# First stage of an attention and mLSTM step kept back and emitted in one stated order; first loads split, prompt compressed with a unit of the samples

## The chip, the cores and the metric

The kernel runs on one core of a Trainium2 chip. The metric is the device time of one execution in microseconds. Five engines work side by side and each takes its instructions in the order in which they stand: PE (matmul, with its weight loads shown as PEld), DVE, ACT, POOL, and SP, which here only issues DMAs. ACT issues some DMAs as well.

## The reference, cut to what matters

A two-layer decoder step: native sparse attention, then an mLSTM. It is done for a prompt of 512 tokens and for 8 samples of one new token with 1024 cached tokens each. Only the start of the first layer matters here: the norm of the input, one projection to keys and values, and the compression of the keys and values of the "cmp" branch into summaries.

```python
SEQ, DEC_BATCH, PAST_LEN, CMP_BLK, CMP_STRIDE = 512, 8, 1024, 32, 16

def compress_branch(rows, pe, w1, b1, w2):
    # block i covers rows [16 i, 16 i + 32); summary = W2 silu(W1 flatten(rows + pe) + b1)
    seg = rows.reshape(B, n_seg, CMP_STRIDE, 2, N_KV_HEADS, HEAD_DIM)
    w1r = w1.reshape(2, CMP_R, CMP_STRIDE, HEAD_DIM, CMP_HID)
    part = einsum('bnrchd,cjrde->bnjche', seg, w1r)
    hid = einsum('cld,clde->ce', pe, w1) + b1
    for j in range(CMP_R):
        hid = hid + part[:, j:j + n_cmp, j]
    return einsum('bnche,ced->bnchd', silu(hid), w2)      # kc for c = 0, vc for c = 1

def nsa_project(h, w_in):
    p = h @ w_in          # q, 4 cached and 2 window key/value groups, gates, z
```

All of it is float32. For the prompt `rows` are its own 512 projected rows, for the samples 1024 rows from pages of the cache.

## The kernel before

Every float32 product is made of three products of the faster format: each operand is split into `hi` (a rounding copy, mostly on ACT) and `lo` (operand minus `hi`, `lo_of`, line 310, on DVE or POOL), and `mm3` (lines 313 to 315) adds `whi*xhi`, `whi*xlo` and `wlo*xhi` in one PSUM bank. So no product can be finished before both splits are there.

The 520 tokens (512 of the prompt and 8 samples) are two column halves `c` of 260. The first stage has these parts:

- **Loads and norm.** ACT issues the first weight tile and both halves of x (`x_t`); `split_x` (371, 372) writes `hhi` and `hlo` for each of eight kt and multiplies by the norm's weight; the squares `sq` (647 on POOL, 649 on ACT) are summed over partitions by a product with `ones` (650), sixteen in all. `rms_factor` makes `rr` from the sum.
- **Key and value tiles.** `kv_tile(i)`, i = 0 to 11: 24 matmuls of 260 columns for each half c, into the two `mm` banks, scaled by `rr` (534) into `kvt`. Weights come through `load_w` (whi, wlo).
- **Sample units.** `cmp_unit(b, c)`, sample b = 0 to 7, keys (c = 0) or values (c = 1): eight pages of the cache by SP (`praw`, three buffers), split into `phi` and `plo` in two parts k, and 48 matmuls of 256 columns with the two halves of w1 (`w1h`, `w1l`) into an `s` bank; then a sigmoid on ACT, `hs`, and a second product (516) that is made during the next unit. `load_w1` loads w1, splits it and sums `acc` over sixteen small DVE instructions (449, 451), from which the bias `hcst` comes.
- **The prompt's compression.** `cmp_prompt_pack` (565) packs `xp` out of two key or value tiles; `cmp_prompt(c)` splits it (574) and makes 48 matmuls of 128 columns into a `t` bank. c = 0 stands after the seventh sample unit, c = 1 after the last.
- **End.** `gates`, `cmp_out`, and then the second stage, which begins with `q_tile`.

In this stage the order is written out for SP alone: it issues in the order of the code. On PE, DVE, ACT and POOL a scheduler of the language places the instructions. Later stages are recorded and emitted in an order given by tables of numbers. Which engine makes a `lo` is set by strings, one letter for each:

```python
LO_W1 = "GGGG"
LO_PG = "VVVVVVVVVVVVVVVVVVVVVVGVVVVVVVVV"
SQX = "SGSGSGSGSGSGSGSS"
```

Of the kernel before, what the change touches and what calls it, by code (L numbers as in the profile page):

```python
# [9 lines left out]
F32 = mybir.dt.float32  # L10
# [8 lines left out]
CH = 260  # L19
# [30 lines left out]
FIRST = 11  # L50
# [130 lines left out]
)  # L181
KSC = float(np.float32(512.0 ** -0.5))
# [52 lines left out]

def const_layout():
# [31 lines left out]
def step_kernel(ctx, tc, ap):  # L268
    nc = tc.nc
    V, S, G, PE, SP = nc.vector, nc.scalar, nc.gpsimd, nc.tensor, nc.sync  # L270

    E = {"V": V, "G": G, "S": S}
    mctx0 = ctx.enter_context(ExitStack())
    mctx0.enter_context(tc.manual_schedule(engines={mybir.EngineType.SP}))
    const = ctx.enter_context(tc.tile_pool(name="const", bufs=1))
    wctx = ctx.enter_context(ExitStack())
    wp = wctx.enter_context(tc.tile_pool(name="wstream", bufs=2, side="right"))
    ps = ctx.enter_context(tc.tile_pool(name="ps", bufs=1, space=PSUM))
# [89 lines left out]
    def split_x(c, kt, xs, li):  # L368

        nwc = nw[:, li, kt:kt + 1]  # L370
        S.activation(hhi[c][:, kt], xs, AF.Copy, scale=nwc)  # L371
        return V.scalar_tensor_tensor(hlo[c][:, kt], xs, nwc, hhi[c][:, kt].bitcast(F32),  # L372
                                      op0=OP.mult, op1=OP.subtract)
# [12 lines left out]
    kvp = l0.enter_context(tc.tile_pool(name="kvp", bufs=1))  # L386
# [16 lines left out]
    hp_ = hctx.enter_context(tc.tile_pool(name="hp", bufs=1, side="right"))  # L403
# [31 lines left out]
    def load_w1(c, after=None):  # L435
        acc = cp.tile([128, 128], F32, name="acc", tag="acc")
        w1[c] = []
        for j in range(2):
            hi = cp.tile([128, 8, 128], F32R, name="w1h", tag="w1h", bufs=3)
            lo = cp.tile([128, 8, 128], F32R, name="w1l", tag="w1l", bufs=3)  # L440
            w1[c].append((hi, lo))
            raw = wp.tile([128, 8, 128], F32, name="wraw", tag="wraw", bufs=WRAW)
            SP.dma_start(raw, ap["w1"][:, c, j])
            S.activation(hi, raw, AF.Copy)
            lo_of(lo, raw, hi, E[LO_W1[2 * c + j]])
            with tc.issue_after(after) if after else nullcontext():
                for r in range(8):
                    if j == 0 and r == 0:
                        V.tensor_scalar(acc, raw[:, r], pe[:, c, j, r:r + 1], None, op0=OP.mult)
                    else:  # L450
                        V.scalar_tensor_tensor(acc, raw[:, r], pe[:, c, j, r:r + 1], acc, op0=OP.mult, op1=OP.add)
# [4 lines left out]

# [6 lines left out]
    def pages(row, u, dst, col, n):  # L463

        for i in range(8):
            v = SP.value_load(pt[0:1, row, u * 8 + i:u * 8 + i + 1], min_val=0, max_val=79)
            SP.dma_start(dst(i), ap["cache"][bass.ds(v, 1), :, col:col + n].rearrange("o p f -> (o p) f"))

    def cmp_unit(b, c):
# [4 lines left out]
        parts = {}  # L474

        def split(k):
# [3 lines left out]
            rv = raw[:, :, k * 128:(k + 1) * 128].rearrange("p g (x s) -> p x g s", s=8)  # L480
# [2012 lines left out]
```

## Time and profile before

| | |
|---|---|
| runs, us | 1149.37, 1151.88, 1156.47; median 1151.88 |
| profiled execution, us | 1150.31, its span 1148.6 |
| mean granted PE clock | 0.976 |
| PE, PEld, DVE, ACT, POOL busy | 93%, 82%, 71%, 54%, 23% of the span |
| first product of a q tile | at 226.8 us |

The profile is one execution. Its page gives the busy share of each engine, then the span in 40 slices of 28.7 us with the busy share in tenths and the clock that PE was granted. Other answers of the trace give the busy time in a stretch, groups of instructions by source line, waits ("A <- B" is the time in which A was idle until B was done), single instructions in order of time, and the DMA engines' load.

### The profile page before, as it was taken

To read this page: it belongs to the slowest core of one execution; us is meant where nothing else is said; L and a number is where in the kernel's file an instruction comes from. 1 tells how busy PE (TensorE), PEld (TensorE's weight loads), DVE (VectorE), ACT (ScalarE), POOL (GpSimd) and SP (SyncE) were. 2 spreads that over 40 slices of the span, in tenths; PEclk is the share of its full clock that TensorE was granted. 3 is DMA by queue.
4 is the path that set the end of the run, shared out by engine and by line. 5 is a ranking of instruction groups with operands and counts; after the bars stand their busy time and mean duration, and the time that the engine had idled before them with its cause. 6 is when DMAs were issued, how large, how long until landed. Compare 5 with 4: busy or idle time off the path is not lost.

```text
span 1148.6 us, 24240 instructions
## 1 busy us (share of the span) xinstructions
PE 1071.7 (93%) x8673; PEld 939.2 (82%) x8673; DVE 812.1 (71%) x1970; ACT 616.7 (54%) x1304; POOL 262.8 (23%) x298
## 2 busy tenths in 40 slices
PE   5899999999999899999899998989989999999985
PEld 4899999999988767778889988779956687877885
DVE  5675564488468888875776667676665778778786
ACT  5533444434567777763444444567655656655644
POOL 5021212042300100002341221221231333322111
PEclk9998999999999999999999999899998999999998
DMA  6544354114433613456344442668788788969522
GB/s 213 169 152 156 121 164 157 38 56 130 127 100 117 195 55 115 122 170 202 127 136 133 163 139 75 238 203 298 243 274 293 218 276 257 349 224 325 171 79 88
DMA packets 124754, 197.20 MB, mean 172 GB/s; under 512 B 16205, under 2 KB 66254, under 8 KB 124378
## 3 DMA queue, kind: packets, MB, share of 16 engines
q1 hardware_dynamic: 115930, 180.52, 48.8%
q10 hardware_dynamic: 8704, 15.13, 3.7%
q8 instruction: 68, 1.11, 0.4%
q14 instruction: 52, 0.43, 0.1%
HBM read 145.89 MB, written 58.10 MB: 178 GB/s over the span
## 4 chain that ended last, share of the span: by engine, by line
PE 32%; DVE 9%; DMA 8%; issue 3%; ACT 3%; SPq 1%; DVEq 0%; POOL 0%; ACTq 0%; POOLq 0%
PE mm L313 7%; PE mm L315 7%; PE mm L314 7%; PE s L2050 3%; DMA wraw<-in_m_in 3%; DMA zd<-zt 3%; PE d L1686 2%; ACT whi L333 1%; DMA wraw<-in_m_out 1%; DVE wlo L310 1%; PE t L2035 1%; PE mm L2025 1%; DVE sacc L358 1%; DVE VT L1458 1%; DVE hlo L372 1%
## 5 line engine op out<-in xcount | busy, mean ns | idle before, releaser
L313 PE MATMUL mm<-hhi,whi 128*128 128x260 f32 (+1 forms) x976 | 284.3, 291 | 18.2 <-ACT hhi L371 10.6
L315 PE MATMUL mm<-hhi,wlo 128*128 128x260 f32 (+1 forms) x976 | 279.6, 287 | 3.6 <-DVE wlo L310 3.5
L314 PE MATMUL mm<-hlo,whi 128*128 128x260 f32 (+1 forms) x976 | 279.5, 286 | 0.0
L313 PEld LDWEIGHTS mm<-hhi,whi 128*128 128x128 f32 (+1 forms) x976 | 185.8, 190 | 26.7 <-ACT hhi L371 10.6
L310 POOL TENSOR_TENSOR wlo<-wraw,whi 128x1024 fp32r<-128x1024 f32 (+2 forms) x57 | 117.1, 2054 | 336.2 <-ACT whi L333 160.6
L315 PEld LDWEIGHTS mm<-hhi,wlo 128*128 128x128 f32 (+1 forms) x976 | 185.8, 190 | 5.3 <-DVE wlo L310 5.1
L314 PEld LDWEIGHTS mm<-hlo,whi 128*128 128x128 f32 (+1 forms) x976 | 185.8, 190 | 0.5
L333 ACT ACTIVATE whi<-wraw 128x1024 fp32r<-128x1024 f32 (+2 forms) x60 | 59.5, 992 | 102.6 <-DMA wraw<-in_m_in 39.8
L1705 DVE SCALAR_TENSOR_TENSOR cs<-t,wk,cs 128x512 f32<-128x512 f32 x128 | 88.4, 743 | 17.1 <-PE t L1678 13.2
L1119 ACT ACTIVATE s<-s,mn 128x512 f32<-128x512 f32 (+3 forms) x128 | 71.3, 560 | 26.5 <-DVE mn L1114 25.1
L1700 ACT ACTIVATE cs<-cs,SBC 128x1024 f32<-128x1024 f32 x64 | 70.9, 1143 | 15.7 <-PE d L1686 15.1
L314 PE MATMUL s<-plo,w1h 128*128 128x256 f32 x256 | 73.7, 288 | 4.5 <-DVE plo L310 4.5
L313 PE MATMUL s<-phi,w1h 128*128 128x256 f32 x256 | 76.0, 297 | 0.0
L310 DVE TENSOR_TENSOR wlo<-wraw,whi 128x1024 fp32r<-128x1024 f32 (+1 forms) x44 | 48.9, 1112 | 36.4 <-ACT whi L333 30.3
L315 PE MATMUL s<-phi,w1l 128*128 128x256 f32 x256 | 72.8, 284 | 0.0
L313 PE MATMUL mm<-uh,whi 128*128 128x260 f32 x224 | 66.1, 295 | 0.3 <-ACT sq L2160 0.2
L1114 DVE CUSTOM_DVE_ANT_0 s<-s,D 128x512 f32<-128x512 f32 (+3 forms) x128 | 59.4, 486 | 8.5 <-PE s L1107 7.6
L310 DVE TENSOR_TENSOR plo<-praw,phi 128x1024 fp32r<-128x1024 f32 x31 | 40.3, 1299 | 35.2 <-ACT phi L483 33.0
L315 PE MATMUL mm<-uh,wlo 128*128 128x260 f32 x224 | 63.6, 284 | 0.0
L314 PE MATMUL mm<-ul,whi 128*128 128x260 f32 x224 | 63.5, 284 | 0.0
L314 PEld LDWEIGHTS s<-plo,w1h 128*128 128x128 f32 x256 | 48.9, 191 | 5.6 <-DVE plo L310 5.1
L1106 PE MATMUL s<-KA,qst 128*128 128x256 f32 (+3 forms) x128 | 48.3, 383 | 4.3 <-ACT pt L1153 2.5
(473 smaller groups left out, 2728.1 us busy)
## 6 DMA issues: line engine op xcount, KB each, us to landing
cs<-in_state_C SPq DMA_DIRECT2D x64, 512.0 KB, 5.4
o_cs<-cs SPq DMA_DIRECT2D x64, 512.0 KB, 4.4
praw<-in_cache SPq DMA_DIRECT2D x128, 128.0 KB, 2.3
dk<-in_cache SPq DMA_DIRECT2D x128, 128.0 KB, 2.3
wraw<-in_m_in SPq DMA_DIRECT2D x32, 512.0 KB, 4.5
wraw<-in_m_out SPq DMA_DIRECT2D x32, 256.0 KB, 3.9
wraw<-in_w_kv SPq DMA_DIRECT2D x11, 512.0 KB, 3.5
wraw<-in_w_q SPq DMA_DIRECT2D x8, 512.0 KB, 3.6
```

The costliest lines, as they stand in the source:

```text
L310: (eng or V).tensor_sub(out, src, hi.bitcast(F32))
L313: PE.matmul(out, whi, xhi, start=start, stop=False)
L314: PE.matmul(out, whi, xlo, start=False, stop=False)
L315: PE.matmul(out, wlo, xhi, start=False, stop=stop)
L333: S.activation(hi, raw, AF.Copy)
L1106: PE.matmul(p[:, 0:n], q[:, h2, i * 128:(i + 1) * 128], KA[:, kh, o:o + n], start=True, stop=False)
L1114: V.tensor_tensor_reduce(s[:, 0:n], X["p", key][:, 0:n], D0[:, 384 - 128 * i:512], SLOPES[4 * kh + g], CLAMP, op0=OP.add, op1=OP.min, accu ...
L1119: S.activation(s[:, 0:n], s[:, 0:n], AF.Exp, scale=-1.0, bias=X["mn"][:, h2, br:br + 1], accum_out=X["sm"][:, h2, br:br + 1])
L1686: PE.matmul(D["pn_", hd][32 * kt:32 * kt + 32], qz[:, kt, b], cts[2 * k + kh][:, i], start=b == 0, stop=b == 7)
L1700: S.activation(ct, ct, AF.Copy, scale=SBC[:, hd, 0, b:b + 1])
L1705: V.scalar_tensor_tensor(ct[:, i], D["pb_", k], D["wk_", hd][:, 2 * kh + i, b:b + 1], ct[:, i], op0=OP.mult, op1=OP.add)
L2050: PE.matmul(st_out(hd, j), ct[:, ks], X["q"][:, 128 * j:], start=kt == 0 and j < 3, stop=kt == 3, skip_group_check=True)
```

## The change

The first stage is recorded, cut into pieces (an instruction, or the matmuls of one bank up to a cut), and emitted at its end in the order of a table of 878 numbers, `CALLS0`, on all five engines. The 129 pieces in a second table, `MOVED0`, change engine: a rounding copy goes from ACT to DVE or back, a subtraction, product or sum from DVE to POOL or back. x and the first weight tile are loaded in halves of four kt, some by ACT and some by SP, and the first tile's products are cut by kt, each triple a piece of its own. The squares of the second column half are first added up, so that one product with `ones` is left of eight. `load_w1` is called for one half at a time. `cmp_prompt` is gone: the units b = 3 (c = 0) and b = 6 (c = 1) take the prompt's `xp` along as 128 more columns, in four parts k of two rounds each.

```diff
+CALLS0 = (
+    7, 0, 2, 22, 3, 1, 10, 19, 6, 177, 12, 18, 20, 17, 5, 29, 25, 124, 23, 4, 26, 9, 24, 35, 30, 27, 11, 36, 31,
...
+class Rec:
+    def add(self, eng, m, a, k):
+        b = a[0].base if eng == "PE" else None
+        if b is not None and self.open is b and self.pieces[-1][0] == "PE":
+            self.pieces[-1][1].append((m, a, k))
+            return
+        self.pieces.append((eng, [(m, a, k)], self.label))
+        self.open = b
...
+    def run(self, engines, order=None, swap=()):
...
+        for n in order:
+            e, calls, _ = self.pieces[n]
+            for m, a, k in calls:
+                if not m:
+                    a[0]()
+                elif n in swap:
+                    swapped(engines, e, m, a, k)
+                else:
+                    getattr(engines[e], m)(*a, **k)
...
+def swapped(engines, e, m, a, k):
+    if m == "activation":
+        engines["DVE"].tensor_copy(a[0], a[1])
+    elif m == "tensor_copy" and e == "DVE":
+        engines["ACT"].activation(a[0], a[1], AF.Copy)
+    else:
+        getattr(engines["POOL" if e == "DVE" else "DVE"], m)(*a, **k)
...
-            wkv[0] = load_w(ap["w_kv"][0], 8, q=S, eng=V)
-        S.dma_start(x, ap["xT"][:, :, c * CH:(c + 1) * CH])
+    for k, q in ((0, S), (1, SP)):
+        ks = slice(4 * k, 4 * k + 4)
+        q.dma_start(raw0[:, ks], ap["w_kv"][0][:, ks])
+        S.dma_start(xc[0][:, ks], ap["xT"][:, ks, 0:CH])
+    for k, q in ((0, S), (1, SP)):
+        ks = slice(4 * k, 4 * k + 4)
+        q.dma_start(xc[1][:, ks], ap["xT"][:, ks, CH:NTOK])
...
-    def cmp_unit(b, c):
+    def cmp_unit(b, c, xp=None):
+        nr, nc_ = (2, 384) if xp is not None else (4, 256)
...
+                for r in range(2):
+                    q = 2 * k + r
+                    rv = raw[:, :, q * 32:(q + 1) * 32].rearrange("p g (x s) -> p x g s", s=8)
...
+                rv = xp[:, 2 * k:2 * k + 2].rearrange("p r h s -> p r (h s)")
...
-            for r in range(4):
-                q = slice(256 * r + j, 256 * r + j + 256)
-                mm3(po[:, 0:256], w1[c][j][0][:, 4 * k + r], w1[c][j][1][:, 4 * k + r], hi[:, q], lo[:, q],
+            for r in range(nr):
+                q = slice(nc_ * r + j, nc_ * r + j + nc_)
+                mm3(po[:, 0:nc_], w1[c][j][0][:, nr * k + r], w1[c][j][1][:, nr * k + r], hi[:, q], lo[:, q],
...
+        if xp is not None:
+            hidden(HP[:, c, :, 0:31], po[:, 256:384].rearrange("p (h t) -> p h t", h=4)[:, :, 0:31], c, [128, 4, 31])
...
-    def cmp_prompt(c):
...
-            PE.matmul(pss[:, :CH], ones, sq, start=kt == 0, stop=kt == 7)
+            if c == 0:
+                PE.matmul(pss[:, :CH], ones, sq, start=kt == 0, stop=kt == 7)
+                R.cut()
+            elif kt:
+                G.tensor_add(acc, acc, sq)
+            else:
+                acc = sq
+        if c:
+            PE.matmul(pss[:, :CH], ones, acc, start=True, stop=True)
...
-            if b == 7:
-                cmp_prompt(0)
...
-    cmp_prompt(1)
...
+    with tc.manual_schedule(engines=every):
+        R.run(NE, CALLS0, MOVED0)
```

Every instruction of the changed kernel passes through one recording line, 407, so its rows all bear that line and are told apart by their tiles.

PE at the very start, before (hhi_93 and hlo_95 are the split x of the first column half, sq its squares):

```order
L313 MATMUL mm<-hhi_93,whi 128x260
L650 MATMUL s<-sq,ones 128x260 x4
L314 MATMUL mm<-hlo_95,whi 128x260
L315 MATMUL mm<-hhi_93,wlo 128x260
L313 MATMUL mm<-hhi_93,whi 128x260
L650 MATMUL s<-sq,ones 128x260 x2
L314 MATMUL mm<-hlo_95,whi 128x260
L315 MATMUL mm<-hhi_93,wlo 128x260
```

and now (hhi_124 and hlo_131 are the first column half, hhi_149 and hlo_154 the second):

```order
L407 MATMUL s<-sq,ones 128x260 x4
L407 MATMUL mm<-hhi_149,whi 128x260
L407 MATMUL mm<-hlo_154,whi 128x260
L407 MATMUL mm<-hhi_149,wlo 128x260
L407 MATMUL mm<-hhi_124,whi 128x260
L407 MATMUL mm<-hlo_131,whi 128x260
L407 MATMUL mm<-hhi_124,wlo 128x260
```

Both column halves are now worked on in turn, kt by kt: four kt of both, then the last four squares, then the other four kt, then the second tile whole, and only then the first sample unit.

DVE around the last hlo, ahead of the first sample unit, before (acc belongs to w1, plo to the first unit):

```order
L449 TENSOR_SCALAR acc<-wraw,pe 128x128
L451 SCALAR_TENSOR_TENSOR acc<-wraw,pe,acc 128x128
L350 TENSOR_TENSOR rs_t<-rs_y 128x260
L451 SCALAR_TENSOR_TENSOR acc<-wraw,pe,acc 128x128
L351 SCALAR_TENSOR_TENSOR rs_t<-rs_t,rv 128x260
L372 SCALAR_TENSOR_TENSOR hlo_96<-x_t,nw,hhi_94 128x260
L352 SCALAR_TENSOR_TENSOR rr_97<-rs_t,rs_y 128x260
```

and now, from the first kvt on:

```order
L407 TENSOR_TENSOR kvt<-mm,rr_351 128x260
L407 CAST phi<-praw 128x1024 x2
L407 TENSOR_SCALAR acc<-wraw,pe 128x128
L407 TENSOR_TENSOR kvt<-mm,rr_351 128x260
L407 CAST w1h<-wraw 128x1024
L407 TENSOR_TENSOR plo<-praw,phi 128x1024
L407 TENSOR_TENSOR w1l<-wraw,w1h 128x1024 x2
L407 SCALAR_TENSOR_TENSOR acc<-wraw,pe,acc 128x128
```

The acc instructions, which stood among the last hlo, now stand behind both w1l; the casts phi and w1h were ACT's, and w1l was POOL's.

PE at the prompt's compression for c = 0, before (the last products of a sample unit, then the prompt's in a t bank):

```order
L313 MATMUL s<-phi,w1h 128x256
L314 MATMUL s<-plo,w1h 128x256
L315 MATMUL s<-phi,w1l 128x256
L313 MATMUL t<-phi,w1h 128x128
L314 MATMUL t<-plo,w1h 128x128
L315 MATMUL t<-phi,w1l 128x128
```

and now (a key and value tile, then unit 3 with the prompt's columns):

```order
L407 MATMUL mm<-hhi_124,whi 128x260
L407 MATMUL mm<-hlo_131,whi 128x260
L407 MATMUL mm<-hhi_124,wlo 128x260
L407 MATMUL s<-phi,w1h 128x384
L407 MATMUL s<-plo,w1h 128x384
L407 MATMUL s<-phi,w1l 128x384
```

The 128-column products are gone; the unit of 384 columns stands in eight pieces among tiles and another unit, where a unit of 256 had stood in four.

More of the change, by code (lines that the diff above doesn't have):

```diff
@@ L433, in step_kernel, with load_w1 @@
     w1 = {}
[L435 to L451, printed above, removed]
+    accs = {}
+    def load_w1(c, j):
+        hi = cp.tile([128, 8, 128], F32R, name="w1h", tag="w1h", bufs=3)
+        lo = cp.tile([128, 8, 128], F32R, name="w1l", tag="w1l", bufs=3)
+        w1.setdefault(c, []).append((hi, lo))
+        raw = wp.tile([128, 8, 128], F32, name="wraw", tag="wraw", bufs=WRAW)
+        SP.dma_start(raw, ap["w1"][:, c, j])
+        S.activation(hi, raw, AF.Copy)
+        lo_of(lo, raw, hi, E[LO_W1[2 * c + j]])
+        if j == 0:
+            accs[c] = cp.tile([128, 128], F32, name="acc", tag="acc")
+        acc = accs[c]
+        for r in range(8):
+            if j == 0 and r == 0:
+                V.tensor_scalar(acc, raw[:, r], pe[:, c, j, r:r + 1], None, op0=OP.mult)
+            else:
+                V.scalar_tensor_tensor(acc, raw[:, r], pe[:, c, j, r:r + 1], acc, op0=OP.mult, op1=OP.add)
+        if j == 0:
+            return
         pc = xb()
@@ L500, in cmp_unit @@
                 split(k)
-            part(k, j, n == 0, n == 3)
+            part(k, j, n == 0, n == len(order) - 1)
+            R.cut()
             if n == 1:
@@ L532, in kv_tile @@
             po = mmb()
-            proj(po[:, :CH], w, hhi, hlo, c)
+            for kt in range(8):
+                mm3(po[:, :CH], w[0][:, kt], w[1][:, kt], hhi[c][:, kt], hlo[c][:, kt], kt == 0, kt == 7)
+                if i == 0:
+                    R.cut()
             V.tensor_mul(t[:, c * CH:(c + 1) * CH], po[:, :CH], rr[c])
@@ L568, in step_kernel @@
     V.memset(HP[:, :, :, 31:32], 0.0)
-    def cmp_prompt(c):
-        hi = cw.tile([128, 1026], F32R, name="phi", tag="phi")
-        lo = cw.tile([128, 1026], F32R, name="plo", tag="plo")
-        xp = XP[c].rearrange("p r h s -> p (r h s)")
-        S.activation(hi[:, 0:1024], xp, AF.Copy)
-        lo_of(lo[:, 0:1024], xp, hi[:, 0:1024])
-        S.activation(hi[:, 1024:1026], ones[:, 0:2], AF.Copy)
-        S.activation(lo[:, 1024:1026], ones[:, 0:2], AF.Copy)
-        po = xb()
-        pv = po[:, 0:128].rearrange("p (h t) -> p h t", h=4)[:, :, 0:31]
-        for j in range(2):
-            for r in range(8):
-                q = slice(128 * r + j, 128 * r + j + 128)
-                mm3(po[:, 0:128], w1[c][j][0][:, r], w1[c][j][1][:, r], hi[:, q], lo[:, q],
-                    j == 0 and r == 0, j == 1 and r == 7)
-        hidden(HP[:, c, :, 0:31], pv, c, [128, 4, 31])
     VT0 = cp.tile([128, 2, 8, 64], F32, name="VT0")
@@ L639, in step_kernel @@
     for c in range(2):
+        R.at("norm", c)
         pss = sb()
+        acc = None
         for kt in range(8):
-            lo = split_x(c, kt, xc[c][:, kt], 0)
-            if 8 * c + kt == FIRST:
-                first = lo
-            sq = cw.tile([128, CH], F32, name="sq", tag="hs")
+            split_x(c, kt, xc[c][:, kt], 0)
+            sq = cw.tile([128, CH], F32, name="sq", tag="sq0" if c and not kt else "hs", bufs=1 if c and not kt else 2)
             if SQX[8 * c + kt] == "G":
```

218 lines of the change are left out of this document (163 added, 55 removed), and 46 rows, old and new, of tables (CALLS0, MOVED0).

## The prediction

> **What bounds the kernel now.** I read the page first: which engine is busy, and where in the span.
>
> ```profile
> PE 1071.7 (93%) x8673; PEld 939.2 (82%) x8673; DVE 812.1 (71%) x1970; ACT 616.7 (54%) x1304; POOL 262.8 (23%) x298
> PE   5899999999999899999899998989989999999985
> PEclk9998999999999999999999999899998999999998
> ```
>
> PE is the bound nearly everywhere; in the first eight slices (28.7 us each), the stage that the change rewrites, the first is half empty and the fourth has a lower clock. Next the busy time of these places by stretch (columns: length, then PE, PEld, DVE, ACT, POOL busy with counts, clock, DMA share, GB/s).
>
> ```profile
> 0.00:10.00 10.00, 0.00 (x0) 0.00 (x0) 1.29 (x2) 3.62 (x3) 5.32 (x9) 1.00 0.81 266
> 10.00:20.00 10.00, 8.30 (x28) 5.39 (x29) 6.88 (x16) 8.11 (x21) 3.14 (x5) 1.00 0.72 247
> 20.00:30.00 10.00, 7.28 (x48) 6.21 (x46) 9.86 (x17) 5.81 (x13) 6.48 (x6) 1.00 0.36 113
> 30.00:40.00 10.00, 7.32 (x47) 7.12 (x48) 8.62 (x21) 3.01 (x9) 2.39 (x1) 0.83 0.58 171
> 40.00:60.00 20.00, 19.96 (x160) 19.31 (x159) 11.33 (x15) 11.69 (x28) 0.21 (x2) 1.00 0.55 165
> 102.00:104.00 2.00, 0.74 (x7) 0.59 (x5) 1.93 (x5) 1.06 (x3) 0.00 (x0) 1.00 0.92 277
> 104.00:106.00 2.00, 1.22 (x11) 1.22 (x12) 1.93 (x5) 1.34 (x4) 0.00 (x0) 1.00 0.50 171
> 106.00:108.00 2.00, 2.00 (x13) 2.00 (x12) 1.91 (x6) 0.00 (x0) 0.00 (x0) 0.59 0.34 112
> 108.00:116.00 8.00, 8.00 (x39) 8.00 (x39) 2.56 (x3) 2.05 (x6) 0.00 (x0) 0.50 0.21 65
> 116.00:118.00 2.00, 2.00 (x16) 2.00 (x16) 0.51 (x3) 0.00 (x0) 0.00 (x0) 0.85 0.01 4
> ```
>
> Until 40 us PE has done 123 matmuls where 20 us of full work hold 160; from 20 to 40 us DVE, not PE, is the busy one. At 102 to 106 us PE stands, and then works for some ten us at half clock. The waits name what PE waited for.
>
> ```profile
> PE mm L313 <- ACT hhi L371: 10.6, 1, 10.6
> PE s L314 <- DVE plo L310: 4.2, 1, 4.2
> PE t L453 <- DVE acc L451: 1.2, 1, 1.2
> PE t L314 <- DVE plo L310: 2.0, 1, 2.0
> ```
>
> The first three lie before 40 us; the last is the prompt's compression, at 102.7 us. Behind the stage nothing is reordered: on every engine and queue the instructions stand in the old order. SP's loads are issued in that order too, so I take the rest of the span as shifted whole.
>
> **The change part by part.** The sum is made on the profiled execution, 1150.31 us (span 1148.6).
>
> *Start, loads.* DMA in 40 slices of 1.125 us from the start, and its rate:
>
> ```profile
> DMA  0279999999999813343313333326864348459854
> GB/s 0 41 297 332 333 341 322 364 370 395 381 375 364 283 65 109 127 99 122 111 46 125 114 117 112 127 95 131 344 193 121 106 121 296 128 129 266 321 178 145
> ```
>
> The engines are full from 3 to 15 us at about 350 GB/s; halving a load makes no byte faster, it only puts the needed ones first. Now: first weights, first x (1.06 MB), both halves of w1 from SP, second x. After: half of each x, half weights, the second tile's weights, then the other halves. Ahead of the last half of x lie x 2.1 MB, two weight tiles 1.05, constants 0.3, about four pages 0.5, small ones 0.1: 4.1 MB / 0.35 = 11.7 us after 2.2, so x is complete near 14 us (now 16.25 in the trace). ACT then splits eight kt and squares two, and casts half a tile:
>
> ```profile
> L371 ACT ACTIVATE hhi<-x_t,nw 128x260 fp32r<-128x260 f32 x16 | 7.1, 498 | 4.8 <-DMA x_t<-in_xT 4.8
> L333 ACT ACTIVATE whi<-wraw 128x1024 fp32r<-128x1024 f32 x15 | 15.9, 1059 | 40.2 <-PE mm L314 26.1 <-DMA wraw<-in_w_kv 8.1 <-DMA wraw<-in_w_q 6.0
> ```
>
> 8 x 0.50 + 2 x 0.41 + 0.53 = 5.3 us, less what came early: I take 18.5 us. By then PE has done the first half of tile 0 for both column halves (24 products). It has 72 left of tiles 0 and 1: 16 at the half-clock pitch of 8/39 = 0.205 us and 56 at 0.119 = 10.0, done at 28.5.
>
> *Start, DVE.* What the first sample unit then waits for is DVE.
>
> ```profile
> L451 DVE SCALAR_TENSOR_TENSOR acc<-wraw,pe,acc 128x128 f32<-128x128 f32 x30 | 18.0, 602 | 0.6
> L451 DVE SCALAR_TENSOR_TENSOR acc<-wraw,pe,acc x30: 335/352/2502, 20.3 to 85.8; 128x128 f32<-128x128 f32 x30
> L544 DVE CAST KA<-kvt x8: 420/422/2021, 98.9 to 170.6; 64x512 fp32r<-64x512 f32 x8
> L565 DVE COPY xp<-kvt x16: 364/374/2494, 37.0 to 107.5; 64x256 f32<-64x256 f32 x16
> 42.75 1.22 DVE L310 TENSOR_TENSOR plo<-praw,phi 128x1024 fp32r<-128x1024 f32 x1 [0.37 <-ACT phi L483]
> 60.17 0.43 DVE L534 TENSOR_TENSOR kvt<-mm,rr 128x260 f32<-128x260 f32 x1 [1.38 <-PE mm L315]
> ```
>
> From about 18 us, behind the last hlo, stand: half a wlo 0.6, six squares and adds and six of rms and kvt 12 x 0.42 = 5.0, three casts of 1024, one acc 0.3, plo 1.22, two w1l 2.4. DVE's cast of 1024 has no row: by the KA cast twice 0.42 = 0.84, by the strided xp copy four times 0.37 = 1.5. I take 1.0, nearer the cast; the three make 3.0. Sum 12.5: w1l is ready at 30.5 (28 if casts and loads go well; 34.5 at 1.5 us a cast with one collision as below). The unit's 48 products then take 14 x 0.205 + 34 x 0.119 = 6.9, to 37.4, while DVE does two adds 0.8, fourteen acc 4.9, a cast 1.0, a plo 1.2: 38.4. The second unit runs from there 5.7 us: **192 products at about 45** with a little for its sigmoid's second product. Now, up to 55.0 us (third product of each triple):
>
> ```profile
> L315 PE MATMUL s<-phi,w1l 128*128 128x256 f32 x48 | 14.1, 294 | 0.0
> L315 PE MATMUL mm<-hhi,wlo 128*128 128x260 f32 x18 | 5.2, 289 | 0.0
> ```
>
> 66 triples, 198 products; less six, 192 at 54.3. **Start: -9.0** (bounds -4 and -13), the seven dropped ones-products of the second half included.
>
> *The stall at 102.7 us goes.* The prompt's columns lie in a unit whose xp was packed long before. **-2.0.**
>
> *The half clock after it goes.* 2 x 0.41 + 8 x 0.50 + 2 x 0.15 = **-5.1**, if PE no longer stands before it. In the Trainium skill, "TensorE: Matmul & The Clock Gate", Part 1, the clock halves after an idle window of about 3.4 us and returns after about 3.4 us of work; here a gap of 2.0 us preceded it and it lasted ten. By that page the gap would be too short to be its cause, and this term would be 0 (total 1137); the first rival below takes that case.
>
> *The merge.* 96 matmuls of 128 columns go, and 96 grow from 256 to 384. Start to start, first and last of a run:
>
> ```profile
> 221.17 0.23 PE L313 MATMUL t<-phi,w1h 128*128 128x128 f32 x1
> 226.37 0.28 PE L315 MATMUL t<-phi,w1l 128*128 128x128 f32 x1
> 218.80 0.28 PE L314 MATMUL s<-plo,w1h 128*128 128x256 f32 x1
> 221.05 0.28 PE L315 MATMUL s<-phi,w1l 128*128 128x256 f32 x1
> 885.63 0.34 PE L313 MATMUL mm<-Sh,vh 128*128 128x384 f32 x1
> 886.16 0.27 PE L313 MATMUL mm<-Sh,vh 128*128 128x256 f32 x1
> ```
>
> 48 narrow ones in 5.20 us are 0.111 each, 20 of 256 columns 0.118, three of 384 0.177. So 96 x 0.111 - 96 x 0.059 = 10.7 - 5.7 = **-5.0**. Twelve small splits in place of six large ones lie on ACT and DVE beside PE, which has 0.04 us idle from 40 to 60.
>
> *What the stated order costs.* Each engine keeps to it: an instruction that comes late holds all behind it. Casts move from ACT to DVE (26 of 1024 columns), nine plo from DVE to POOL (ten now), wlo and w1l from POOL to DVE; POOL has 17 subtractions of 1024, 16 before. They get in DVE's way:
>
> ```profile
> 60.63 3.69 DVE L565 COPY xp<-kvt 64x256 f32<-64x256 f32 x4
> 61.24 2.43 POOL L310 TENSOR_TENSOR wlo<-wraw,whi 128x1024 fp32r<-128x1024 f32 x1 [8.30 <-ACT whi L333]
> ```
>
> Four copies of 0.37 took 3.69 while POOL ran. The Trainium skill ("SBUF — State Buffer", Who interferes with whom) has such pairs exclude each other for a whole instruction; the row agrees, and by it ten plo on POOL could hold DVE for 24 us. From below the cost is nothing (DVE has 8 us free in 40 to 60), from above three episodes like that at 102 us, 3 x 7.1 = 21. I take **+3**, nearer nothing.
>
> At the stage's end PE still has the first q tile's matmuls between the last transposes, as now: 0.
>
> Sum: 1150.3 - 9.0 - 2.0 - 5.1 - 5.0 + 3 = 1132.2. The median of the runs is 1.6 above the profiled execution; I say **1133**.
>
> **The rivals.**
> (1) The half clock comes elsewhere, or the start gains only the lower bound. For it: ten us at half clock after only 2.0 us. Against: at PE's other gaps between 40 and 240 us, all under 1 us, the clock stayed at 1.00. 1133 + 5.1 = 1138; with the start at -4, 1143. Chance 0.20.
> (2) Slower: PE waits for POOL's plo in the sample units, each wait a stop of 2.0 and a half clock of 5.1. Ten plo stand there; it decides from the third (no gain left), and five in place of the allowance make 1133 - 3 + 5 x 7.1 = 1165. Against: one subtraction more on POOL than before, and DVE free for 8 us in 40 to 60. Chance 0.08.
> (3) The gain is hidden: a transfer behind the stage arrives when it did. Against: SP issues in order. 1150; chance 0.04.
> (4) The start reaches -13 and order costs nothing: 1126 or less. Chance 0.08.
>
> **How the numbers follow.** The forecast, 1126 to 1140, has 0.60. The range 1122 to 1150 leaves out most of (2), little else. One per cent, 11.5 us, is about what a measurement here can tell from no change: faster takes the forecast, (4) and a third of (1), 0.75; the same the rest of (1), (3) and a little of (2), 0.18; slower 0.07.
>
> **What would show it.** PE with 192 products near 45 us; no second row at clock 0.50; no 128-column product with w1h, 96 at 384 columns 0.177 apart; the first q product near 209 instead of 227. Wrong: PE idle in DVE's or POOL's name between 45 and 200 us, or DVE still full at 50.

## The result, and the profile after

| | before | after |
|---|---|---|
| median, us (4 runs each, side by side) | 1150.62 | 1134.60 |
| lowest to highest | 1148.99 to 1156.47 | 1132.13 to 1135.48 |
| profiled execution, its span | 1150.31, 1148.6 | 1135.48, 1132.8 |
| mean granted clock | 0.976 | 0.980 |
| last of the first 192 products of units and tiles starts | 54.1 | 46.9 |
| first q product, the stage's end | 226.8 | 211.1 |
| from there to the end of the span | 921.8 | 921.6 |

The ratio after to before is 0.985, with a 95% interval of 0.981 to 0.989. The last two rows of the table say where the time came from: all of it lies ahead of the first q product, 7.2 us in the start and 8.5 us between there and the stage's end. (The 192 products are read here at the start of the last one, 54.1 for before; the prediction read 54.3 off the 198th. They are the same amount of work in another mix: in before 137 of them are the units' and 55 the tiles', in after 96 and 96.) The page of the kernel after:

```profile
PE 1058.4 (93%) x8563; PEld 929.7 (82%) x8563; DVE 813.6 (72%) x1988; ACT 602.0 (53%) x1326; POOL 277.2 (24%) x306
PE   6999999999998999999999998999999999999985
PEclk9999999999999899999999998999999999999988
```

Matmuls fell by 110, and PE's busy time by 13.3 us: 96 are the narrow ones, 14 the seven dropped products with `ones`, each of which stands as two matmuls in the trace (32 for sixteen before, 18 for nine now). The first slice rose from 5 to 6 tenths, and the lower clock of the fourth slice is gone. The stretches of the start:

```profile
0.00:10.00 10.00, 3.19 (x7) 2.10 (x8) 3.04 (x8) 4.91 (x11) 4.98 (x8) 1.00 0.83 268
20.00:30.00 10.00, 7.39 (x60) 6.98 (x59) 9.86 (x15) 3.06 (x9) 4.71 (x3) 1.00 0.67 208
30.00:40.00 10.00, 8.03 (x64) 7.56 (x63) 9.53 (x24) 2.81 (x6) 1.09 (x3) 0.99 0.38 124
40.00:60.00 20.00, 20.00 (x155) 19.95 (x155) 13.90 (x23) 8.52 (x26) 3.12 (x4) 0.92 0.65 199
108.00:116.00 8.00, 7.52 (x62) 7.28 (x61) 4.59 (x8) 2.19 (x5) 2.72 (x2) 1.00 0.45 130
```

From 20 to 40 us PE made 124 matmuls instead of 95, but DVE is full there, at 9.86 and 9.53 of ten, and the clock was halved once more, in the row from 40 to 60. At 108 to 116, where before ran at 0.50 with 39 matmuls, there are 62 at 1.00. PE's waits, the first four up to 50 us, the last two from 50 to 230:

```profile
PE s L407 <- ACT sq L407: 8.6, 4, 6.0
PE mm L407 <- DVE kvt L407: 2.6, 2, 1.3
PE t L407 <- DVE acc L407: 1.4, 1, 1.4
PE s L407 <- DVE plo L407: 0.5, 1, 0.5
PE s L407 <- DVE plo L407: 2.0, 1, 2.0
PE t L407 <- DVE hs L407: 1.3, 1, 1.3
```

The first is the loads, seen through the squares (10.6 us before, in the name of `hhi`). The wait of 4.2 us for the first unit's `plo` is down to 0.5. New is `mm <- DVE kvt` in the start: PE waits for a free `mm` bank, which DVE empties into `kvt`. What DVE did then, and POOL in the first row:

```profile
24.19 2.81 POOL L407 TENSOR_TENSOR plo<-praw,phi 128x1024 fp32r<-128x1024 f32 x1
24.70 2.39 DVE L407 TENSOR_SCALAR acc<-wraw,pe 128x128 f32<-128x128 f32 x1
27.01 0.42 DVE L407 TENSOR_TENSOR kvt<-mm,rr 128x260 f32<-128x260 f32 x1
27.35 0.68 DVE L407 CAST w1h<-wraw 128x1024 fp32r<-128x1024 f32 x1
29.08 2.35 DVE L407 TENSOR_TENSOR w1l<-wraw,w1h 128x1024 fp32r<-128x1024 f32 x2
39.47 3.14 DVE L407 TENSOR_TENSOR plo<-praw,phi 128x1024 fp32r<-128x1024 f32 x1
```

One `acc` of 0.3 us took 2.39, to the moment at which POOL's subtraction ended, with `kvt` behind it; one `plo` of 1.22 took 3.14. The one stop of PE in the middle of the stage is at 186.4:

```profile
184.45 1.06 ACT L407 ACTIVATE whi<-wraw 128x1024 fp32r<-128x1024 f32 x1 [5.03 <-DMA wraw<-in_w_q]
185.59 2.34 POOL L407 TENSOR_TENSOR wlo<-wraw,whi 128x1024 fp32r<-128x1024 f32 x1 [2.93 <-ACT whi L407]
186.39 1.83 DVE L407 TENSOR_TENSOR plo<-xp,phi 128x256 fp32r<-128x256 f32 x1 [4.35 <-ACT phi L407]
188.37 0.42 PE L407 MATMUL s<-plo,w1h 128*128 128x384 f32 x1 [1.96 <-DVE plo L407]
188.62 0.34 PE L407 MATMUL s<-phi,w1l 128*128 128x384 f32 x1
188.80 0.34 PE L407 MATMUL s<-phi,w1h 128*128 128x384 f32 x1
```

The first two rows belong to the first q tile, the second stage's, which the table does not order: there a scheduler places the instructions, and it put this cast inside the first stage. ACT waited 5.03 us for the cast's weights, with the merged unit's `phi` behind it, and the q tile's `wlo` on POOL then stretched DVE's `plo` to 1.83. So the stop is not the stated order's own. The last two rows show products of 384 columns 0.18 us apart.

### The profile page after: what moved, and what is told of

The parts are those of the page before. It is cut to its first block, busy times and chain, and to the rows that moved or that the text cites. A ratio compares the mean times of both kernels' runs of the same rounds, so it can differ in the third digit from the quotient of the medians.

```text
span 1132.8 us, 24065 instructions
## 1 busy us (share of the span) xinstructions
PE 1058.4 (93%) x8563; PEld 929.7 (82%) x8563; DVE 813.6 (72%) x1988; ACT 602.0 (53%) x1326; POOL 277.2 (24%) x306
## 4 chain that ended last, share of the span: by engine, by line
PE 28%; DMA 10%; DVE 9%; issue 3%; ACT 3%; POOL 1%; SPq 1%; DVEq 0%; ACTq 0%; POOLq 0%
PE mm L407 18%; PE t L407 4%; PE s L407 4%; DMA zd<-zt 4%; DMA wraw<-in_m_in 4%; PE d L407 2%; ACT whi L407 1%; DVE x L407 1%; DMA wraw<-in_m_out 1%; DVE VT L407 1%; DVE sacc L407 1%; DVE zt L407 1%; SPq L407 1%; DVE wlo L407 1%; DVE CT L407 1%
## 5 line engine op out<-in xcount | busy, mean ns | idle before, releaser
L407 POOL TENSOR_TENSOR wlo<-wraw,whi 128x1024 fp32r<-128x1024 f32 (+1 forms) x52 | 106.6, 2051 | 255.7 <-ACT whi L407 239.0
L407 ACT ACTIVATE whi<-wraw 128x1024 fp32r<-128x1024 f32 (+1 forms) x98 | 88.9, 908 | 115.6 <-PE mm L407 53.2
L407 PE MATMUL s<-phi,w1h 128*128 128x256 f32 (+1 forms) x256 | 77.9, 304 | 0.7 <-DVE hs L407 0.5
L407 PE MATMUL s<-plo,w1h 128*128 128x256 f32 (+1 forms) x256 | 74.8, 292 | 2.5 <-DVE plo L407 2.5
L407 DVE TENSOR_TENSOR wlo<-wraw,whi 128x1024 fp32r<-128x1024 f32 (+2 forms) x50 | 54.6, 1093 | 30.7 <-ACT whi L407 30.3
L407 PE MATMUL s<-phi,w1l 128*128 128x256 f32 (+1 forms) x256 | 74.7, 292 | 0.0
L407 PEld LDWEIGHTS s<-phi,w1h 128*128 128x128 f32 x256 | 49.0, 192 | 1.5 <-PE mm L407 0.7
```

The lines of the kernel that those rows point to most:

```text
L407: return f(*[real(x) for x in a], **{n: real(x) for n, x in k.items()})
```

## The experiments

All kernels keep the order of before behind the first q product, but for a few instructions at the seam, so each is read by two marks of its one trace, the 192 products and the first q product, beside the median of its runs. "Before" was timed with each group; the rest of the span alone varied from 913 to 926 us between executions.

| kernel | 192 products | first q | median (runs) | before beside it | ratio, 95% |
|---|---|---|---|---|---|
| before | 54.1 | 226.8 | | | |
| after | 46.9 | 211.1 | 1134.6 (4) | 1150.6 | 0.981 to 0.989 |
| merge alone | 53.0 | 217.7 | 1144.6 (10) | 1145.4 | 0.997 to 1.004 |
| merge, split loads | 54.6 | 221.6 | 1150.1 (7) | 1145.4 | 1.004 to 1.010 |
| prompt earlier | 52.8 | 218.7 | 1144.2 (10) | 1145.4 | 0.997 to 1.004 |
| prompt in wide products | 53.1 | 220.9 | 1144.1 (10) | 1145.4 | 0.998 to 1.004 |
| after, again | 45.9 | 209.3 | 1134.1 (8) | 1149.5 | 0.983 to 0.991 |
| after, no engine changed | 48.2 | 215.2 | 1134.6 (4) | 1149.5 | 0.982 to 0.996 |
| other order of the start | 42.8 | 209.8 | 1127.5 (4) | 1149.5 | 0.978 to 0.992 |
| and two stops removed | 42.0 | 205.2 | 1126.8 (4) | 1149.5 | 0.977 to 0.989 |
| and a third | 42.9 | 204.7 | 1121.4 (6) | 1146.9 | 0.975 to 0.983 |
| after, loads tile by tile | 49.9 | 215.0 | 1133.1 (8) | 1146.9 | 0.983 to 0.991 |
| long stop, wide products | 42.3 | 215.0 | 1137.6 (1) | | |
| long stop, narrow products | 41.9 | 229.7 | 1147.6 (1) | | |

**The parts, without the stated order.** The kernel before, with the units b = 3 and b = 6 of 384 columns and without `cmp_prompt`; the scheduler goes on placing the instructions.

```diff
-            cmp_unit(b, 0)
+            cmp_unit(b, 0, XP[0] if b == 3 else None)
...
-            if b == 7:
-                cmp_prompt(0)
...
-        cmp_unit(b - 8, 1)
+        cmp_unit(b - 8, 1, XP[1] if b == 14 else None)
...
-    cmp_prompt(1)
```

> The kernel before with the merge alone: the prompt's columns ride in units 3 and 6 as 128 more, cmp_prompt is gone; the scheduler places everything and the first loads are as before. Theory (the terms of the prediction add up): merge -5.0, stall at 102.7 us -2.0, half clock after it -5.1, so 12 us faster, about 1138.5 against 1150.6; no stop of PE near 102 us and no ten us at clock 0.50 there. Rival 1 (the half clock comes elsewhere): 5 to 7 us faster, 1144 to 1146. Rival 2 (only the stated order makes the merged unit run without waits; its eight pieces each wait for a split): under 3 us faster, 1148 or more, with PE idle in the name of phi or plo inside the units of 384 columns.

The stage ended at 217.7, and of the 9.1 us against before 1.1 lay ahead of the 192 products. From there to the first q product lie 164.7 us; less a stop of 2.6 and 1.7 for half clock, PE needed 160.4. The kernel below with the prompt one unit earlier keeps the narrow products and needs 165.4 (165.9 less a stop of 0.5). That is the merge, 5.0. But the scheduler put the merged unit's `phi` late:

```profile
PE s L313 <- ACT phi L499: 2.6, 1, 2.6
```

The stop lay at 61 us, and half clock followed it: 12 matmuls in 3.42 us where 30 would stand.

```profile
61.86:65.27 3.41, 1.48 (x9) 1.48 (x10) 2.47 (x5) 0.72 (x2) 0.82 (x1) 1.00 0.39 125
65.27:68.69 3.42, 3.42 (x12) 3.42 (x11) 0.76 (x2) 1.08 (x5) 0.00 (x0) 0.50 0.54 157
```

2.6 and 1.7 of the gain were given back, and the medians do not differ: of the three expectations the second rival came nearest, under 3 us and PE idle in the name of `phi` at a unit of 384 columns. Next the same with the first loads in halves, as after has them, still without the stated order:

```diff
+    for k, q in ((0, S), (1, SP)):
+        ks = slice(4 * k, 4 * k + 4)
+        q.dma_start(raw0[:, ks], ap["w_kv"][0][:, ks])
+        S.dma_start(xc[0][:, ks], ap["xT"][:, ks, 0:CH])
...
+        S.activation(hi0[:, ks], raw0[:, ks], AF.Copy)
+        lo_of(lo0[:, ks], raw0[:, ks], hi0[:, ks])
```

> The kernel before with the merge and with the split first loads, still placed by the scheduler: what is left to the kernel after is then the stated order, the changed engines and the one ones-product. Theory (the start gains from order and engines as much as from loads): the loads give 2 of the 7.3 us, so 1136.5, with after at 1134.6; DVE still full from 20 to 40 us. Rival 1 (loads are the start's whole gain): 1131 to 1132, faster than after. Rival 2 (loads give nothing without the order): 1138.5, as the merge alone.

None of the three expectations held: the start was 1.6 us later than with the merge alone, and the median 0.4 to 1.0% above before's.

```profile
PE s L314 <- DVE plo L310: 7.1, 3, 4.6
PE s L313 <- ACT phi L509: 2.7, 1, 2.7
```

PE waited 7.1 us in the sample units for `plo`, three times; before waited 4.5 there, twice. So halved loads bring nothing under the scheduler's order.

**The stall and the half clock.** First the narrow products of c = 0 one unit earlier, ahead of the second `load_w1`:

```diff
+                cmp_prompt(0)
+            if b == 6:
                 load_w1(1)
-            if b == 7:
-                cmp_prompt(0)
```

> The kernel before with cmp_prompt(0) called one unit earlier, where DVE has no KA casts and KB subtractions of a key tile in front of the prompt's plo; the 96 products of 128 columns stay. Theory (the half clock follows from the stop): the 2.0 us stop and the 5.1 us of half clock go, 7 us faster, 1143.5, and the 48 narrow products run at 0.111 us each. Rival 1 (narrow products bring the half clock, not the stop): 2 us faster, 1148.6, a row at clock 0.50 over the narrow products though PE did not stop. Rival 2 (the wait moves along with the call): within 1 us, PE idle before a t product in DVE's name.

The stall shrank from 2.0 to 0.5 us, no half clock followed, and the stage ended at 218.7, 8.1 earlier, of which 1.3 lay in the start; the narrow products ran 0.111 apart at full clock. Yet the median was before's, not the 7 us lower that was expected. The second kernel keeps the stall and makes the prompt's products wide (254 columns, of which half go unused):

```diff
-            for r in range(8):
-                q = slice(128 * r + j, 128 * r + j + 128)
+            for r in (0, 1, 2, 3, 4, 5, 7, 6):
+                n = 128 if r == 7 else 254
+                q = slice(128 * r + j, 128 * r + j + n)
```

> The kernel before with the prompt's products widened from 128 to 254 columns (84 of the 96; the added columns are not used): the stop of 2.0 us before them should stay, only what follows it is other. Theory 1 (the stop sets off ten us of half clock whatever comes next): 84 x 0.007 = 0.6 us slower, 1151, and a half clock of ten us again. Theory 2 (one short window of half clock, some 3.4 us as at 31.5 us, but narrow products, which do 128 columns in 0.213 us where the others do 260 in 0.217, keep it going until they are done): half clock of about 3.4 us, so 5.1 - 1.7 - 0.6 = about 3 us faster, 1148, though the products are twice as large. Should the stop bring no half clock at all this time, that is a third outcome: 1146 in that execution.

The stall was there, 1.8 us, and no half clock came behind it, the third outcome of the expectation. What sets the two apart shows when both traces are cut at the moments at which the clock changes. They lie on a grid of 3.41 us, whose offset differs from execution to execution. Before:

```profile
102.95:106.36 3.41, 1.58 (x14) 1.58 (x15) 3.28 (x8) 2.04 (x5) 0.00 (x0) 1.00 0.62 223
106.36:109.78 3.42, 3.42 (x18) 3.42 (x18) 3.15 (x6) 0.00 (x0) 0.00 (x0) 0.50 0.36 117
109.78:113.19 3.41, 3.41 (x18) 3.41 (x18) 0.00 (x0) 0.00 (x0) 0.00 (x0) 0.50 0.28 80
113.19:116.60 3.41, 3.41 (x18) 3.41 (x18) 1.48 (x2) 2.05 (x6) 0.00 (x0) 0.50 0.00 0
116.60:120.02 3.42, 3.42 (x30) 3.42 (x30) 0.43 (x1) 0.00 (x0) 0.00 (x0) 1.00 0.01 2
```

and the kernel with wide products:

```profile
101.58:104.99 3.41, 1.85 (x15) 1.86 (x16) 3.29 (x7) 1.91 (x5) 0.00 (x0) 1.00 0.68 238
104.99:108.40 3.41, 3.41 (x32) 3.41 (x30) 2.94 (x6) 0.00 (x0) 0.00 (x0) 1.00 0.36 118
```

The same stall left PE busy for 1.58 us of one stretch of the grid in the one (46%) and for 1.85 us in the other (54%); the first lost the clock in the next stretch, the second did not. By itself this pair doesn't say whether the place of the stall or the wider products behind it kept the clock. Another stop does: ahead of the merged unit's late products of 384 columns, five traces have the same stop of 1.8 to 2.0 us. Where PE stood for at most 41 or 50% of one stretch (after repeated, after), no half clock followed; where it stood for 53, 61 and 71% (no engine changed, other order, loads tile by tile), half clock came. Over the fourteen traces, from 12 us on, half clock followed each of the 87 stretches at full clock in which PE stood for at least 55%, and 32 of the 161 in which it stood for 30 to 55%; of the some 4150 in which it stood less, 6, all at one place of a later stage, with products of 8 columns. So the half clock of before may well be a matter of where its stall falls; no second trace of before was taken to show it. It would fit the medians: 55 runs of before had mean clocks from 0.966 to 0.986 and times from 1156.8 to 1134.6, with a correlation of -0.80. The profiled execution, at 1150.3, is above their median of 1146.5.

**After again, and without changed engines.** The second kernel keeps the order and empties the table of pieces that change engine.

```diff
 MOVED0 = (
-    29, 37, 53, 66, 67, 71, 74, 75, 82, 87, 91, 100, 101, 112, 132, 133, 137, 157, 165, 179, 199, 200, 202, 211,
...
 )
```

> The kernel after once more, beside the same executions of before as the experiments below. Theory (a half clock follows a stop only where most of the stop falls into one stretch of a fixed clock grid of 3.41 us, so it comes in some executions and not in others): the 2.0 us stop of before brought it in one of two traces with that stop, so on average 2.6 of the 5.1 us counted; before without it ends its stage at 221, with it at 227, after at 209 to 211; the times differ by about 13, 1132 against 1145. Rival (the half clock of before is there in every execution): 16 us, 1129 to 1130 against 1145, or before near 1150 again.

> The kernel after with the stated order, but no piece changes its engine (an empty second table): all casts back on ACT, w1l and wlo on POOL, plo on DVE. Theory (the order gives the start, the swaps only shift work between engines that PE seldom waits for): stage end within 4 us of 211, time within 4 us of after. Rival 1 (the order was made for the swapped engines; each engine keeps to it and waits): PE waits for ACT's or POOL's pieces in many units, stage end above 220, no gain left over the kernel before. Rival 2 (swaps harm, by DVE and POOL getting in each other's way): stage end below 208.

After repeated: 209.3, with half clock again in the start (38.4 to 41.8) and the same stop of 1.97 us, without half clock behind it. Its median lies 15.4 us under that of the ten runs of before beside it, nearer to the rival's 16 than to the theory's 13; the interval, 10 to 20 us, allows both. Without the changes of engine the start was 1.3 to 2.3 later and the stage's end 4 to 6 (3.4 us of half clock at 191.4 among it), but the median was the same. The 4.1 us to after's trace just miss the theory's 4. The order, not the engines, is most of the gain; the engines are worth a few microseconds of the stage that these runs do not resolve in the whole time.

**Removing what was lost in the start.** Another order of the pieces that stand between tile 0's last products and the second unit; two `phi` of the sample units go back to ACT, and the `plo` that POOL made at 24 us, two sums of squares and the third tile's `wlo` go to DVE.

```diff
-    74, 131, 58, 195, 75, 187, 59, 196, 78, 60, 99, 188, 110, 79, 234, 83, 152, 90, 86, 132, 155, 137, 134, 133,
+    82, 186, 74, 131, 58, 195, 75, 187, 59, 196, 132, 137, 134, 139, 78, 60, 99, 188, 110, 133, 138, 100, 234,
+    152, 235, 236, 155, 79, 101, 111, 151, 135, 140, 83, 112, 150, 90, 86, 154, 87, 91, 153, 136, 102, 103,
...
```

> The kernel after with another order up to about 48 us, where PE stands 1.3 us before each half of the second tile and 1.9 us before the second sample unit: the casts phi of the first unit go back to ACT, kvt and both w1l come before the sums acc, the cast and plo of the second unit come in the middle of the acc, wlo of the third tile goes to DVE. Theory (DVE's order, not the loads, sets the start): 192 products at 41.5 to 42.5 us instead of 46.9, PE standing under 1 us at the second unit and so no half clock there, stage end 206, about 5 us faster than after. Rival (the next wait takes its place: the third tile's weights, whose buffer the acc sums hold, or the pages of the third unit, which SP issues 1.1 us apart): 192 products early, but a stop of 2 us or more at the third tile or unit, gain 2 us or less.

The 192 products stood at 42.8, 4.1 earlier than after; 41.5 to 42.5 had been expected. But this time the stop of 1.96 us that after has at 186 was followed by half clock. Cut at the grid, after and then this kernel:

```profile
183.24:186.65 3.41, 2.95 (x23) 2.48 (x20) 0.26 (x1) 1.97 (x5) 1.06 (x1) 1.00 0.58 211
186.65:190.07 3.42, 1.70 (x12) 1.73 (x13) 2.32 (x3) 0.96 (x3) 1.28 (x1) 1.00 0.26 99
```

```profile
182.98:186.39 3.41, 1.36 (x6) 1.14 (x7) 2.58 (x3) 0.80 (x4) 2.06 (x1) 1.00 0.11 17
186.39:189.81 3.42, 3.42 (x17) 3.42 (x16) 0.49 (x2) 1.59 (x5) 0.13 (x1) 0.50 0.34 137
```

In after the stop is shared by two stretches, here one has it whole. The stage ended at 209.8, not at the expected 206; that the median still fell by 7 us lies mostly behind the stage, where this execution took 913.1 us and after 921.6. Next the first q tile's cast is kept behind a late piece of the stage (826), and a product that waited for `hs` goes behind a tile's products:

```diff
-        S.activation(hi, raw, AF.Copy)
+        with tc.issue_after(after) if after else nullcontext():
+            S.activation(hi, raw, AF.Copy)
...
-        w = load_w(ap["w_q"][hp * 4 + g], 8, eng=E[LO_Q[hp * 4 + g]])
+        w = load_w(ap["w_q"][hp * 4 + g], 8, eng=E[LO_Q[hp * 4 + g]], after=None if qst else R.mark)
```

> As the last one, and two late stops taken away: the cast of the first q tile's weights, which ACT made at 184 us after waiting 5 us for their load with three phi behind it (and POOL's wlo of it in DVE's way), is held until the prompt's last split is made; one second product whose hs came 1.3 us late stands behind a tile's products. Theory: stops of 2.0 and 1.3 us go, stage end 203, 8 us faster than after. Rival (the wait moves to the q tile): the stage's last unit ends at 203 but PE stands before the first q product, gain of the start alone.

The stops at 135 and 186 were gone, the stage ended at 205.2 (203 had been expected), and one stop of 1.2 us was left, for the ones that ACT writes at the end of each `plo`, which stood behind the copies of `xp`. Those two pieces moved ahead of the copies:

```diff
-    222, 306, 221, 163, 172, 164, 165, 199, 201, 202, 242, 200, 240, 241, 239, 238, 198, 243, 250, 245, 244,
+    222, 214, 306, 221, 223, 163, 172, 164, 165, 199, 201, 202, 242, 200, 240, 241, 239, 238, 198, 243, 250,
...
```

> The last one, with the small copies of ones into plo of the third unit put ahead of ACT's copies of xp, behind which they stood while PE waited 1.2 us at 51.5 us. Theory: that stop goes, stage end 204 instead of 205.2, about 1 us faster than e9, 9 us faster than after (1125 against 1134), 20 faster than before. Rival: the first q products wait for the end's transposes anyway, stage end still 205.

That stop went too, and the stage ended at 204.7. At 1121.4 us this version beats both kernels, before by 2.1%; of the 13 us to after's median the stage holds 4.7 to 6.5 in the profiled executions; the rest lies behind it, where nothing was changed, and its cause is open.

```profile
20.00:30.00 10.00, 9.32 (x67) 8.90 (x67) 9.36 (x17) 5.44 (x12) 0.00 (x0) 0.90 0.61 200
30.00:40.00 10.00, 9.54 (x78) 9.27 (x77) 8.30 (x19) 3.22 (x8) 0.21 (x2) 1.00 0.51 167
```

POOL has 0.2 us of work from 20 to 40 us, DVE 2.3 us of room, and PE makes 145 matmuls where after made 124. (The 0.90 is half clock from 18.5 to 21.9 us.)

**What the order of the first loads is worth.** After, with the first tile's weights, then the halves of x for one column half and then the other, ahead of the second tile's weights:

```diff
-    7, 0, 2, 22, 3, 1, 10, 19, 6, 177, 12, 18, 20, 17, 5, 29, 25, 124, 23, 4, 26, 9, 24, 35, 30, 27, 11, 36, 31,
+    0, 2, 22, 3, 1, 6, 7, 8, 9, 10, 12, 17, 19, 11, 18, 20, 177, 124, 5, 29, 25, 23, 4, 26, 24, 35, 30, 27,
...
```

> The kernel after with its order of work, but the first loads issued tile by tile, as before: both halves of the first weights, both of the first x, both of the second x, then the second tile's weights. Theory (the loads' order is a small part of the start, for the engines' order is what bounds it): x complete about when it was, the first product 1 to 2 us later, 192 products at 47 to 48.5 us. Rival (the split and reordered loads are what the start lives on): 192 products at 51 us or later, stage end 214 or more.

The 192 products stood at 49.9, 3 to 4 later than in the two traces of after, and 1.7 of that is a half clock that lasted two stretches instead of one. Less that, the loads' order is worth 1.3 to 2.3 us in the start, within the theory. The stage ended at 215.0, past the rival's mark of 214, but 1.7 of that is one more half clock, behind the stop at 189; the median, 1133.1, is no higher than after's.

**The price of a stop, and of narrow products behind it.** In the best version a unit waits 8.1 to 8.3 us at 124, for a subtraction that POOL makes four times; in the second kernel that unit's 48 products of 256 columns are 96 of 128. Each kernel was run once.

```diff
+                if (b, c, k) == (0, 1, 0):
+                    def slow():
+                        for _ in range(4):
+                            lo_of(lv, rv, hv, G)
+                    R.fn("POOL", 9.6, 0, slow)
```

```diff
+                n = 128 if (b, c) == (0, 1) else nc_
+                for o in range(0, nc_, n):
+                    q = slice(nc_ * r + j + o, nc_ * r + j + o + n)
```

> e10 with a stop made on purpose: the first plo of unit 0 for the values (at about 118 us) is computed four times over on POOL, so that PE stands some 6 us or more; the products behind the stop have 256 columns as always. Theory (a stop that fills more than half of a 3.41 us stretch of the clock grid halves the clock for the next stretch, and wide products let it return after one): clock 0.50 from before the end of the stop to at most one stretch after it, loss behind the stop under 1.8 us. Rival (what follows does not matter): the same length as in the next kernel.

> The same stop, but the 48 products of 256 columns behind it are issued as 96 of 128 columns. Theory (products of 128 columns, which take as long as those of 260 at half clock, do not bring the clock back): clock 0.50 until the last of them is done, 96 x 0.213 = 20 us, as after the stop at 102.7 us in the kernel before, where it lasted through the 42 narrow products and one stretch more. Rival 1: clock back after one stretch, as with the wide ones, the 96 products then at 0.111 each, 10.7 us. Rival 2 (ten us whatever comes): back after three stretches.

Wide:

```profile
127.40:130.82 3.42, 0.00 (x0) 0.00 (x0) 3.37 (x3) 0.00 (x0) 3.34 (x2) 0.50 0.10 29
130.82:134.23 3.41, 2.12 (x10) 2.12 (x11) 1.27 (x1) 0.00 (x0) 3.41 (x2) 0.50 0.12 40
134.23:137.64 3.41, 3.41 (x16) 3.23 (x16) 0.68 (x1) 1.80 (x4) 1.56 (x3) 0.50 0.85 280
137.64:141.05 3.41, 3.41 (x30) 3.39 (x30) 1.21 (x3) 0.68 (x1) 0.00 (x0) 1.00 0.38 123
```

and narrow:

```profile
131.11:134.52 3.41, 2.65 (x13) 2.65 (x13) 0.73 (x1) 0.00 (x0) 3.02 (x2) 0.50 0.20 68
134.52:151.59 17.07, 17.07 (x81) 16.89 (x80) 3.02 (x4) 3.22 (x7) 1.37 (x2) 0.50 0.24 83
155.00:158.41 3.41, 3.41 (x18) 3.41 (x18) 0.00 (x0) 0.08 (x1) 0.00 (x0) 0.50 0.02 5
158.41:161.83 3.42, 3.42 (x27) 3.31 (x27) 0.61 (x2) 1.51 (x7) 2.02 (x2) 1.00 0.00 0
```

With wide products the clock came back 5.5 us after the stop ended, behind one stretch full of work; one stretch at most had been expected. With narrow ones PE was full at half clock from 134.5 on, and yet the clock stayed there until 158.4: through all the narrow products, which ended at 153.9, to the end of the first stretch that was full of products of 260 columns. That is 30.7 us of half clock against 10.2. The stage ended 14.7 us later, of which 96 x 0.111 - 48 x 0.118 = 5.0 are the narrow products' own, and the other 9.7 the clock's. The ten us of before are the same thing: two stretches of narrow products, then one of wide ones.

## Why the prediction was right, and where its steps were off

The predicted 1133 stands against 1134.6, and the predicted stage's end near 209 against 211.1 and 209.3. By its own steps:

- **Start, -9.0: measured -7.2.** x was complete as said (the `hhi` of its last halves start at 13.57, predicted 14). PE resumed at 18.4 (18.5 said). The next step failed: tiles 0 and 1 were done at 30.5 instead of 28.5. I had put PE at its pitch through the 72 products and all DVE work beside it, but two of those tile banks waited for `kvt` on DVE: 1.34 us behind the squares and the rms that make `rr`, and 1.26 behind two casts and the `acc` of 2.39. The sixteen products put in at half clock ran at full clock, which saved 1.4 of it. After it w1l was done at 31.4 (30.5 said) and the second `plo` at 39.3 (38.4). The cast, guessed at 1.0, took 0.68; by luck a collision, which the sum held in its worse bound only, made up for it. Then half clock from 39.9 to 43.3 cost 1.7 more. The other order of the start, at 42.8, shows that the lower bound of the term, -13, was nearly within reach: -11.3.

- **The stall, -2.0: right.** No wait lies there any more; the prompt moved one unit earlier alone had left 0.5 of it.

- **The half clock behind it, -5.1: right in this pair of executions, not as a term of the median.** The trace of before had it, many of its executions may not: the two experiments that lost it, one of them with the stall kept, have the median of before beside them. The forecast of the time doesn't rest on this, for it starts from the execution that had the half clock; the size of the gain does, and that it came out at 16.0 is in part luck. The prediction's rule was "if PE no longer stands before it"; a stop of 2.0 us brings it or not, by where it falls. The profiled execution lies 3.8 above the median of 55 runs; against that median after's gain is about 12 (12 runs of it have 1134.3), not the 16.0 of the first two medians. In the Trainium skill, "TensorE: Matmul & The Clock Gate", Part 1, the window of activity runs freely and is about 3.41 us long: the grid in these traces agrees. From that page of the Trainium skill the prediction read that a gap of 2.0 us would be too short; here 1.96 us was long enough when one stretch had it whole, and the measurement decides. The one busy window to come back, which the Trainium skill states there, held for products of 256 columns and more, not for those of 128.

- **The merge, -5.0: right,** shown by itself (165.4 to 160.4, one trace each), and worth nothing in the median where the scheduler made PE wait for the merged unit.

- **The stated order, +3: right in size, by another path.** PE stood 3.9 us between the 192 products and 211, against 0.9 in before outside the stall, and the first q product came 1.26 instead of 0.41 us behind the last unit's: +3.9. The prediction named POOL's `plo` as the danger; PE waited for none of them. What it feared of POOL came through other instructions. The stop of 1.28 at 136 was for an `hs` on DVE; ahead of it a DVE cast took 2.48 instead of 0.42 beside POOL's `wlo`, and a DVE copy 1.18 instead of 0.16 beside another subtraction. Half of the 3.9, the 1.96 at 186, was the second stage's cast among the first's instructions, with POOL's `wlo` of it in DVE's way. The prediction had seen that behind the stage nothing is reordered, and did not look at what a scheduler puts back across the seam. Its own sign of being wrong, PE idle in DVE's name between 45 and 200 us, showed at these two stops.

The terms as measured make -7.2 - 2.0 - 5.1 - 5.0 + 3.9 = -15.4, and the stage's end moved by 15.7. The start came out 1.8 short and the order 0.9 dearer. Two slips of the sum are small: 1132.2 and 1.6 make 1133.8, not 1133, and the half-clock pitch of 0.205, read as 8 us over all 39 matmuls that touch that stretch, is 0.213 from start to start.

Of the rivals, the first came true by half: half clock returned in the start, in one stretch and for 1.7 us. The second did not come: PE waited for no `plo` of POOL in the units, and its longest stop there was 2.0. In the Trainium skill, "SBUF — State Buffer", Who interferes with whom, a DVE and a POOL instruction that need the port pair they share exclude each other. 2.39, 3.14 and 1.83 us for DVE instructions of 0.28, 1.22 and about 0.4 agree. But most such delays cost little: POOL made 15 subtractions of 1024 columns between 50 and 211 us, and PE stood 3.9 us there in all. The third, a hidden gain, is excluded by the rest of the span, 921.8 and 921.6. The fourth, 1126 or less, was open to another order, as the last versions show.

What the experiments leave open: how often executions of before have their half clock (only profiled executions show it), and in part why the rest of the span varies by 13 us with the same order. The fourteen traces show where it varies: behind the first q product PE stands for 52.0 to 61.2 us and works for 24.5 to 38.3 us at half clock, and the rest of the span less the standing and half of the half-clock work is 846.6 to 849.8 us in all of them. Why the standing differs from one execution to the next stays open.

## What to carry to other kernels

A split of loads or a merge of products pays only as far as the order of every engine lets it: here both were worth nothing in the median under the scheduler, and with a stated order the stage gave 15.7 us, with a better one 22. Before a stop of PE or the clock behind it is put into a sum, read the granted clock of several executions; one profile may show a half clock that other runs don't have. At the seam between a stated order and code that a scheduler places, look at which side's instructions stand first on each engine: one cast with a late load held a whole unit.

## What the runs showed of the hardware

- In these traces the granted clock changes only on a grid of 3.41 us, which lies differently in each execution. A stop of 1.8 to 2.0 us can cost its own length, or 1.7 us more in the stretch behind it; where PE stood for 55% of a stretch or more it always did, 87 times of 87.
- Products of 128 columns at half clock were 0.213 us apart, those of 256 as much, those of 260 0.216, and the narrow ones did not bring the clock back in 22 us of work without a stop. At full clock, narrow products 0.111 apart did not lose it in 5 us. That the clock goes by the columns that pass in a stretch, and not by whether PE has an instruction, would explain both (an estimate from these pitches: 600 columns a us did not bring it back, 1200 did, and 1150 kept it); it was only argued.
- A cast of 128x1024 on DVE took 0.68 us, a little over half of the 1.22 that a subtraction of that size takes there; beside a subtraction on POOL a DVE instruction can last until that one ends, 2.39 us for one of 0.28.
